# The last 15 full loads of a row-mean kernel, each split by partitions over two DMA queues

## The chip, the core and the metric

The kernel runs on one core of a Trainium2 chip. The metric is the time of one execution in device microseconds (us): the lower the better. Times before are given as the median of three executions; a profile is one further execution, recorded by the hardware profiler.

A core has a memory of 128 partitions (SBUF), engines that work on it (VectorE, written DVE in the profile; ScalarE, ACT; GpSimd, POOL; SyncE, SP) and 16 DMA engines that move data between the chip's main memory (DRAM) and SBUF. An engine issues a DMA into its queue and goes on; the DMA reports its end by adding 16 to a semaphore, on which other engines wait.

## The reference

```python
def setup_inputs():
    return {
        "x": np.random.randn(64, 256, 8192).astype(np.float32),
    }

def reference(x: np.ndarray) -> np.ndarray:
    return np.mean(x, axis=2)
```

There are 64 x 256 = 16384 rows of 8192 numbers, 32 KB each, 536.87 MB in all; the result is one mean for each row, 64 KB in all.

## The kernel before, in words

**Tiling.** Each of the 128 partitions owns 128 rows (`OWN`). The rows are laid out in three zones (`ZONE = [95, 17, 16]` rows per partition), inside each of which a partition's rows follow one another in DRAM. A *full load*, numbered g, brings two rows into each partition: a tile of 128 x 16384 numbers, 64 KB for each partition, 8.39 MB. There are 63 such pairs (g = 0 to 62, `NB`), and one last pair that comes in five chunks. Pair g = 0 holds the odd row of zones 0 and 1 and comes in three pieces. `PAIRS0` is 47: g = 1 to 47 come from zone 0, g = 48 to 62 from zones 1 and 2.

**Buffers.** Three buffers (`bufs`, `NBUF = 3`) take the loads in turn; load g goes to buffer g mod 3. So up to three loads are in flight or being reduced.

**SyncE** issues every DMA of the kernel, in this order: the three pieces of g = 0 and the loads 1 and 2 (lines 107 to 114); in a loop of 15 rounds (`ROUNDS`) over the three buffers the loads 3 to 47 (lines 118 to 123), each after `free_sems[b]` says that VectorE has reduced what lay in the buffer, and that semaphore is counted down again; then, unrolled, the 15 loads 48 to 62 (lines 124 to 127), each after a wait on the same semaphore, which is now left to count up; then the five chunks of the last pair (lines 128 to 133) into the first buffer and a small tile `fin`, and at the end the stores of the result (lines 134 to 142).

**VectorE** reduces each landed load by one `tensor_reduce` to two sums per partition in `res`: the first 60 loads in a loop of 20 rounds (lines 165 to 173), in which the wait on `in_sems[b]` counts that semaphore down, and the loads 60 and 61 unrolled (line 178). Load 62 and the chunks are added by `halves` (line 151), which adds the two halves of a row elementwise and accumulates the sum.

**ScalarE** only takes a part of each of the four larger chunks (lines 202 to 207), after that chunk's semaphore. **GpSimd** scales the finished sums by 1/8192 (lines 87 to 99) when VectorE has done load 60 and what follows it up to row 126; the last column is scaled with the last addition.

What sets the order around the change: the loads go through SyncE's one queue in the order of g; a load is issued when VectorE has finished load g - 3; the chunks are issued when load 60 has been reduced; ScalarE's program holds nothing before its work on the chunks.

## Time and profile before

| what | before |
|---|---|
| median of 3 executions | 1243.22 us (1243.2 to 1243.32) |
| the profiled execution | 1243.06 us |
| its span in the trace | 1241.7 us |
| read from DRAM | 536.87 MB, 432 GB/s over the span |
| ScalarE busy | 5.2 us |
| GpSimd busy | 2.9 us |

The span runs from the first to the last recorded instruction; the execution's own time is 1.36 us longer. In the profile a line such as `L168` is the kernel's line 168. A group of instructions is shown with its engine, operation, output and input tile and count, then its busy time in us, the mean in ns of one, and the idle time of the engine just before them with what ended it. `SPq` or `DVEq` stands for an engine's sequencer, which executes waits and issues DMAs. Of three numbers with strokes between them the first is the least, the second the median, the third the largest, in ns for an instruction. In a table by stretches stand the stretch's bounds and length, the busy time of each engine (with the count of instructions), the clock granted to TensorE, which this kernel does not use, the mean busy share of the 16 DMA engines, and what they moved in GB/s.

### The profile page before, as it was taken

Reading aid. Unit: us, or ns where it says so; the run is one execution under the profiler, and the core shown is the slowest. Engines: PE = TensorE matmul, PEld = TensorE weight load, DVE = VectorE, ACT = ScalarE, POOL = GpSimd, SP = SyncE. Lnnn points to the kernel's source line nnn. Section 1 sums busy time; section 2 is a strip of 40 time slices with the busy share of each in tenths; the row PEclk is TensorE's granted clock in tenths of the full one; section 3 lists DMA queues with packets and bytes.
Section 4 is the critical chain, followed back from the end, with each engine's and each line's share of the span. In section 5 each row is a group of like instructions: output and inputs, shape, how many; then the busy total and the mean of one; then the engine's idle time right before and its main releaser. Section 6 shows DMA issues by size and latency. Waiting matters only on the chain. (4 is left out here: it accounts for less than half of the span.)

```text
span 1241.7 us, 549 instructions
## 1 busy us (share of the span) xinstructions
DVE 1084.1 (87%) x76; ACT 5.2 (0%) x9; POOL 2.9 (0%) x9
## 2 busy tenths in 40 slices
DVE  2898988989889898898898988989889898898987
ACT  0000000000000000000000000000000000000001
POOL 0000000000000000000000000000000000000000
DMA  9999999999999999999999999999999999999998
GB/s 405 439 439 439 439 435 410 439 439 439 439 439 433 412 439 439 439 439 439 426 418 439 439 439 439 439 422 422 439 439 439 439 439 422 422 439 439 439 439 374
DMA packets 10512, 536.94 MB, mean 432 GB/s; under 512 B 1552, under 2 KB 1552, under 8 KB 1936
## 3 DMA queue, kind: packets, MB, share of 16 engines
q1 hardware_dynamic: 10512, 536.94, 99.9%
HBM read 536.87 MB, written 0.07 MB: 432 GB/s over the span
## 5 line engine op out<-in xcount | busy, mean ns | idle before, releaser
L168 DVE TENSOR_REDUCE res<-buf 128x16384 f32 x60 | 1033.2, 17220 | 146.5 <-DVEq L167 146.5
L178 DVE TENSOR_REDUCE res<-buf 128x2 f32<-128x16384 f32 x2 | 34.4, 17220 | 4.0 <-DMA buf<-in_x_dram 4.0
L151 DVE CUSTOM_DVE_ANT_0 buf<-buf 128x4096 f32<-128x4096 f32 (+3 forms) x6 | 16.0, 2672 | 5.4 <-DMA buf<-in_x_dram 5.4
L207 ACT ACTIVATE buf<-buf 128x928 f32<-128x928 f32 (+3 forms) x4 | 3.6, 897 | 1233.7 <-DMA buf<-in_x_dram 1233.7
L97 POOL TENSOR_SCALAR scaled<-res 128x94 f32<-128x94 f32 (+2 forms) x3 | 2.4, 784 | 1235.0 <-DVE res L151 1234.8
L207 ACT ACT_TABLE_LOAD x1 | 1.3, 1283 | 0.7 <-PEq L221 0.7
L207 ACT ACTIVATION_READ_ACCUMULATOR buf<-buf 128x1 f32 x4 | 0.7, 187 | 0.0
L151 DVE CUSTOM_DVE_ANT_0 fin<-fin 128x260 f32<-128x260 f32 x1 | 0.4, 429 | 0.3 <-DMA fin<-in_x_dram 0.3
L97 POOL TENSOR_SCALAR ends<-res 128x15 f32<-128x15 f32 x1 | 0.3, 264 | 0.1
L151 DVE DVE_READ_ACCUMULATOR2_ANT res<- 128x1 f32 x3 | 0.3, 84 | 0.0
L151 DVE DVE_READ_ACCUMULATOR2_ANT fin<- 128x1 f32 x3 | 0.2, 81 | 0.0
L221 POOL MEMSET const-bfloat16-1.0<- 128x1 bf16 x1 | 0.1, 102 | 0.0
L221 POOL MEMSET const-uint8-127<- 128x1 uint8 x1 | 0.1, 102 | 0.0
L88 POOL MEMSET fin<- 128x1 f32 x1 | 0.1, 99 | 0.3 <-POOLq L221 0.3
L221 POOL MEMSET const-float32-0.0<- 128x1 f32 x1 | 0.1, 99 | 0.2 <-issue 0.2
L221 POOL MEMSET const-float32-1.0<- 128x1 f32 x1 | 0.1, 99 | 0.0
L151 DVE DVE_READ_ACCUMULATOR2_ANT ends<- 128x1 f32 x1 | 0.1, 82 | 0.0
## 6 DMA issues: line engine op xcount, KB each, us to landing
buf<-in_x_dram SPq DMA_DIRECT2D x1, 4560.0 KB, 32.2
buf<-in_x_dram SPq DMA_DIRECT2D x1, 4096.0 KB, 20.6
buf<-in_x_dram SPq DMA_DIRECT2D x1, 3072.0 KB, 11.4
buf<-in_x_dram SPq DMA_DIRECT2D x1, 2240.0 KB, 37.1
buf<-in_x_dram SPq DMA_DIRECT2D x1, 1024.0 KB, 4.6
buf<-in_x_dram SPq DMA_DIRECT2D x62, 40.3
buf<-in_x_dram SPq DMA_DIRECT2D x1, 768.0 KB, 38.5
buf<-in_x_dram SPq DMA_DIRECT2D x1, 368.0 KB, 39.0
```

The lines of the kernel that those rows point to most:

```text
L88: eng.memset(part(NPART - 1), 0.0).then_inc(part_d, 1)
L97: eng.tensor_scalar(dst, src, inv, None, op0=mybir.AluOpType.mult).then_inc(pool_sem, 1)
L151: eng.tensor_tensor_reduce(ap[:, 0:n], ap[:, 0:n], ap[:, n : 2 * n], scale=scale, scalar=0.0, op0=ADD, op1=ADD, accum_out=to,).then_inc(do ...
L168: eng.tensor_reduce(sums[:, bass.ds(i, 1), b, :], bufs[b][:].rearrange("p (j l) -> p j l", j=2), X, ADD,).then_inc(free_sems[b], 1)
L178: eng.tensor_reduce(res[:, 2 * g : 2 * g + 2], bufs[b][:].rearrange("p (j l) -> p j l", j=2), X, ADD,).then_inc(free_sems[0] if b == 0 els ...
L207: eng.activation(ap, ap, COPY, accum_out=part(c)).then_inc(part_a, 1)
L221: nc = _bacc.Bacc("TRN2", target_bir_lowering=False, num_devices=1)
```

## The change

The 15 loads g = 48 to 62 each become two DMAs. Partitions 0 to 63 are issued by SyncE, as before, partitions 64 to 127 by ScalarE, each after its own wait for the buffer. Both add 16 to the same new semaphore `late_in_sems[b]`, so VectorE waits for multiples of 32; VectorE's releases for these loads go to the new `late_free_sems[b]`. Since constants are waited for there, VectorE's loop is shortened from 20 to 15 rounds (`ROUNDS`), and loads 45 to 62 are unrolled. Loads 0 to 47, the chunks and the stores stay as they are, on SyncE's queue. ScalarE's 15 issues stand ahead of its work on the chunks.

```diff
+        late_in_sems = [sem(f"late_in_sem{i}") for i in range(NBUF)]
+        late_free_sems = [sem(f"late_free_sem{i}") for i in range(NBUF)]
...
         eng = nc.gpsimd
         eng.memset(part(NPART - 1), 0.0).then_inc(part_d, 1)
-        eng.wait_ge(free_sems[0], LOADS0 + 1)
+        eng.wait_ge(late_free_sems[0], LOADS0 + 1)
         eng.wait_ge(owned_sem, 4)
...
         eng = nc.sync
...
         for g in range(PAIRS0 + 1, NB):
             b = g % NBUF
-            eng.wait_ge(free_sems[b], (g - PAIRS0 - 1) // NBUF + 1)
-            eng.dma_start(bufs[b][:], rows_of(first_row(g), 2)).then_inc(in_sems[b], 16)
-        eng.wait_ge(free_sems[0], LOADS0 + 1)
+            eng.wait_ge(late_free_sems[b], (g - PAIRS0 - 1) // NBUF + 1)
+            eng.dma_start(bufs[b][0 : P // 2, :], rows_of(first_row(g), 2)[0 : P // 2, :]).then_inc(
+                late_in_sems[b], 16
+            )
+        eng.wait_ge(late_free_sems[0], LOADS0 + 1)
         two = rows_of(2 * NB, 2)
...
-        with eng.Fori(0, NB // NBUF - 1) as i:
+        with eng.Fori(0, ROUNDS) as i:
             for b in range(NBUF):
                 eng.wait_ge(in_sems[b], 16).then_inc(in_sems[b], -16)
                 eng.tensor_reduce(
...
                 ).then_inc(free_sems[b], 1)
-        for b in range(NBUF):
-            g = NB - NBUF + b
-            eng.wait_ge(in_sems[b], 16)
-            if b < 2:
+        for g in range(ROUNDS * NBUF, NB):
+            b = g % NBUF
+            if g <= PAIRS0:
+                eng.wait_ge(in_sems[b], 16)
+            else:
+                eng.wait_ge(late_in_sems[b], 32 * ((g - PAIRS0 - 1) // NBUF + 1))
+            if g < NB - 1:
                 eng.tensor_reduce(
                     res[:, 2 * g : 2 * g + 2],
                     bufs[b][:].rearrange("p (j l) -> p j l", j=2),
                     X,
                     ADD,
-                ).then_inc(free_sems[0] if b == 0 else owned_sem, 1)
+                ).then_inc(late_free_sems[b] if g < NB - 2 else owned_sem, 1)
             else:
...
         eng = nc.scalar
+        for g in range(PAIRS0 + 1, NB):
+            b = g % NBUF
+            eng.wait_ge(late_free_sems[b], (g - PAIRS0 - 1) // NBUF + 1)
+            eng.dma_start(bufs[b][P // 2 : P, :], rows_of(first_row(g), 2)[P // 2 : P, :]).then_inc(
+                late_in_sems[b], 16
+            )
         for c in range(4):
             eng.wait_ge(chunk_sems[c], 16)
```

More of the change, by code (lines that the diff above doesn't have):

```diff
@@ L83, in bass_global_avg_pool_1d_kernel, with rows_of @@
         part = lambda n: fin[:, LAST + n : LAST + n + 1]
+        def rows_of(n, k):
+            z = 2 if n >= FROM[2] else 1 if n >= FROM[1] else 0
+            return zone[z][:, (n - FROM[z]) * L : (n - FROM[z] + k) * L]
         eng = nc.gpsimd
         eng.memset(part(NPART - 1), 0.0).then_inc(part_d, 1)
-        eng.wait_ge(free_sems[0], LOADS0 + 1)
+        eng.wait_ge(late_free_sems[0], LOADS0 + 1)
         eng.wait_ge(owned_sem, 4)
@@ L102, in bass_global_avg_pool_1d_kernel @@
         eng = nc.sync
-        def rows_of(n, k):
-            z = 2 if n >= FROM[2] else 1 if n >= FROM[1] else 0
-            return zone[z][:, (n - FROM[z]) * L : (n - FROM[z] + k) * L]
         a, z = rows_of(ZONE[0] - 1, 1), rows_of(ZONE[0], 1)
```

## The prediction

> **What bounds the kernel now.** I read the page first: busy times, slices, queues, costliest groups.

> ```profile
> span 1241.7 us, 549 instructions
> ...
> DVE 1084.1 (87%) x76; ACT 5.2 (0%) x9; POOL 2.9 (0%) x9
> ...
> DMA  9999999999999999999999999999999999999998
> ...
> DMA packets 10512, 536.94 MB, mean 432 GB/s; under 512 B 1552, under 2 KB 1552, under 8 KB 1936
> ## 3 DMA queue, kind: packets, MB, share of 16 engines
> q1 hardware_dynamic: 10512, 536.94, 99.9%
> ...
> L168 DVE TENSOR_REDUCE res<-buf 128x16384 f32 x60 | 1033.2, 17220 | 146.5 <-DVEq L167 146.5
> L178 DVE TENSOR_REDUCE res<-buf 128x2 f32<-128x16384 f32 x2 | 34.4, 17220 | 4.0 <-DMA buf<-in_x_dram 4.0
> ```

> VectorE is busy 87% of the span, the DMA engines 99.9%: the transfers set the time. All of them stand in one queue, q1. The packet counts give the size of a packet: 10512 less the 1936 under 8 KB is 8576, which is 67 x 128, that is, the 62 full loads (g = 1 to 62) and five large pieces (three at the start, chunks 0 and 1) at one packet for each partition. So a full load is 128 packets of 64 KB, eight for each of 16 engines.

> Then busy times by stretch, cut at the ends of the loads that the change touches:

> ```profile
> core 0: us, DVE busy (x) ACT busy (x) POOL busy (x), PEclk, DMA share, GB/s
> 22.50:911.30 888.80, 792.11 (x46) 0.00 (x0) 0.00 (x0) 1.00 1.00 434
> 911.30:930.60 19.30, 17.22 (x1) 0.00 (x0) 0.00 (x0) 1.00 1.00 435
> 930.60:1220.20 289.60, 258.30 (x15) 0.00 (x0) 0.00 (x0) 1.00 1.00 433
> 1220.20:1241.70 21.50, 16.44 (x14) 3.96 (x8) 2.62 (x4) 1.00 0.87 366
> ```

> The 15 loads of the change, g = 48 to 62, take 289.60 us, 19.31 each, at a DMA share of 1.00 and 433 GB/s. One 64 KB packet on one engine is 19.31 / 8 = 2.41 us. What follows the last of them is 21.5 us long. And the order of events where the change begins and ends:

> ```profile
> 909.31 270.74 SPq L127 DMA_DIRECT2D buf<-in_x_dram  x15
> 911.37 17.22 DVE L168 TENSOR_REDUCE res<-buf 128x16384 f32 x1 [2.09 <-DVEq L167]
> 930.65 17.22 DVE L168 TENSOR_REDUCE res<-buf 128x16384 f32 x1 [2.06 <-DVEq L167]
> 949.96 17.22 DVE L168 TENSOR_REDUCE res<-buf 128x16384 f32 x1 [2.09 <-DVEq L167]
> ...
> 1200.96 17.22 DVE L178 TENSOR_REDUCE res<-buf 128x2 f32<-128x16384 f32 x1 [2.16 <-DMA buf<-in_x_dram]
> 1220.27 4.42 DVE L151 CUSTOM_DVE_ANT_0 buf<-buf 128x4096 f32<-128x4096 f32 x1 [2.09 <-DMA buf<-in_x_dram]
> ```

> VectorE starts on g = 46 at 911.37, on g = 47 at 930.65, on g = 48 at 949.96, on g = 62 at 1220.27. It idles about 2.1 us before each, waiting for data. (Inside the loop the wait is put on its own sequencer, DVEq; the two unrolled reductions show the same wait as DMA.)

> **The change part by part.** *Issues and waits.* SyncE still issues 15 DMAs here, and ScalarE 15 more.

> ```profile
> L127 SPq DMA_DIRECT2D buf<-in_x_dram x15: 327/328/339, 909.3 to 1179.7; - x15
> ...
> DMA to landing us min/median/max: 40.4/40.5/40.5
> ```

> ```profile
> SPq L127 <- DVE res L168: 284.2, 15, 19.0
> ```

> ```profile
> ACT buf L207 <- DMA buf<-in_x_dram: 1233.7, 4, 1229.0
> ```

> An issue takes 0.33 us and then the load needs 40.5 us to land, since two loads stand ahead of or in it: 2 x 19.31 = 38.6, and 1.8 for getting started and reporting. SyncE waits up to 19.0 us between issues for VectorE. ScalarE does nothing until 1229, so 15 issues of 0.33 to 0.43 us and the waits before them cost nothing: queued behind them stand only the four ACTIVATEs of the chunks (L207), which in program order follow the last issue, and whose data comes later still. If that cover were gone, 15 x 0.43 = 6.5 us of ScalarE would show. VectorE's shorter loop (15 rounds instead of 20), its constant waits and its other semaphores touch sequencer work inside the 2.1 us idle time before each load: nothing. GpSimd waits for the same reduction under another name: nothing. Fifteen more sets of 16 completion packets are 15 more packets per engine, under 512 B each; at the 27.1 GB/s of one engine (64 KB in 2.41 us) at most 0.02 us each, 0.3 us in all.

> *Bytes.* The same 8.39 MB move per load, but in two transfers of 64 partitions, and the trace has no 64-partition transfer of any size. The price is bounded from both sides. Below: a half costs half of a full load, 9.66 us, because only the bytes count; 15 x (2 x 9.66 - 19.31) = 0. A gain beyond that is limited by the share of 1.00: see the third rival. Above: a half costs as much as a full load, 19.31 us, because what is limited is the rate into each set of partitions, and a half load brings each of its partitions the same 64 KB. Then 15 x (2 x 19.31 - 19.31) = 289.6 us.

> I take the upper end. The nearest row is the full load itself: same queue kind, same packets of 64 KB per partition, and a rate that stands at 433 to 435 in every stretch, as a limit of fixed width would leave it. My hypothesis is that this width belongs to the partitions: the lower 64 can take half of it (217 GB/s), the upper 64 the other half. A full load asks both halves equally. A half load asks one, and is as slow as a full one unless the other half load runs beside it on the other engines.

> That last condition decides, so I follow the packets. I assume that a half load too is spread over all 16 engines, four packets on each, and that an engine with work on both queues takes whole packets from them in turn. Up to 909 all engines work one queue through packets of equal length, and 99.9% of 16 x 1241.7 us is filled: 1.2 us idle per engine, less than what the start and the end of the span take (0.7 us pass before the first issue), so no engine is far ahead of another. They enter the new stage in step: all 16 write a ScalarE packet (upper partitions), then all 16 a SyncE packet (lower partitions), each time at half rate, 4.83 us a packet instead of 2.41. Two engines that share one half-width equally finish together and stay together; nothing pulls them apart. Every half load then pays 4 x 2.41 = 9.66 us extra, wherever it falls in the order, and 30 of them pay 289.6.

> [...]

> *Order.* ScalarE's queue is empty when it gets its half of g = 48 at 909, while SyncE's still holds the rest of g = 46 and all of g = 47. So the upper halves run one load ahead: g = 47 shares its turns with the upper halves of 48 and 49 and lands after 4 x (4.83 + 2.41) x 2 = 58 us, near 969 instead of 930. VectorE stands idle meanwhile; that costs nothing while the engines have work, and they have: halves of 48 and 49 are waiting. At the end the last lower half (g = 62) runs alone, at half rate as well. No packet is priced twice, so the sum is not changed by the order.

> *Sum.* Against the profiled execution: span 1241.7 + 289.6 + 0.3 = 1531.6 us. That execution took 1243.06 in all, 1.36 us outside the span, and lies 0.16 below the median of 1243.22; I forecast **1533 us**. In stretches: the 15 loads end near 1510 instead of 1220.2, and the 21.5 us after them stay. The forecast's own range is 1500 (the engines a tenth of a packet out of step, 289.6 x 0.9) to 1560 (each load also shows its 1.8 us start, 15 x 1.8 = 27).

> **The rivals.** *Only the bytes count.* If each engine is limited by itself, or each half lands on eight engines of its own, the two halves side by side take 19.31 us. For: the engines are filled to 1.00, as one would see with that limit too. Against: nothing in the trace, only that the widths of both would have to be equal by accident. The one new wait: g = 47 shares its turns and lands at 930.6 + 19.3 = 949.9; VectorE frees its buffer 17.2 us later, at 967.2, and the queues run dry at 949.9 + 19.3 = 969.2, with 1.8 us needed to start. So at most about 1 us is lost, and VectorE regains its 19.3 us of delay at 2.1 per load over 13 loads. Result 1243 to 1245.

> *Out of step.* The partition limit holds, but one engine of a sharing pair gets ahead, or engines interleave in pieces smaller than a packet. Then engines write to opposite halves and most of the loss vanishes. A floor remains where the two queues don't balance: 12.6 of the 16.8 MB moved beside g = 47 go to the upper half, 57.9 us instead of 38.6, so +19.3; then the lower half of 48 alone, +9.7; the lower half of 62 alone, +9.7. That is 1282; with half of the packets colliding, 1243 + 145 = 1388. For: equal sharing is my assumption, a small bias would add up over 120 packets. Against: the regular 19.3 us steps of VectorE show no drift in the whole span. Range 1262 (one of the two imbalances of 19.3 us only) to 1500.

> *Faster.* A second queue lets an engine fetch the next packet while the first queue's is finishing. Place: the seam between two packets. Price: the slices of the profile move at most 439 GB/s against 433 here.

> ```profile
> GB/s 405 439 439 439 439 435 410 439 439 439 439 439 433 412 439 439 439 439 439 426 418 439 439 439 439 439 422 422 439 439 439 439 439 422 422 439 439 439 439 374
> ```

> At 439 a load takes 19.11 us, 15 save 15 x 0.20 = 3 us: 1240. It decides only if halves don't slow each other at all and there are seams; a share of 1.00 and a chain of full packets leave hardly any (the dips between the 439s are whole packets counted in the next slice).

> **How the numbers follow.** A measurement of this kernel tells about 0.2% (2.5 us) from no change. Chances: forecast (1500 to 1560) 0.53; out of step (1262 to 1500) 0.27; only the bytes count 0.14; faster 0.03; slower than 1560, where two queues also get in each other's way, 0.03. Slower is 0.53 + 0.27 + 0.03 = 0.83, same 0.14, faster 0.03. The range 1262 to 1560 holds the first two, 0.80.

> **What would show it.** In the profile after: a second queue with 15 x 64 = 960 packets of 64 KB and 63 MB; in the stretch of the split loads 215 to 220 GB/s at a DMA share still near 1.00 (packets take 4.8 us, engines are not idle); VectorE's starts 38.6 us apart with some 21.4 us idle, and one idle time near 40 us before g = 47; landing times of the split halves near 77 us from SyncE and 40 to 60 from ScalarE; the last 21.5 us unchanged. A stretch at 433 GB/s with starts 19.3 us apart says that only bytes count. Something between, drifting from 38 to 20 us, says that the engines fall out of step. Idle DMA engines in the stretch would prove the reasoning wrong altogether: then a wait, not a width, is the cause.

## The result, and the profile after

The changed kernel takes 1554.33 us (median of 4; 1553.91 to 1555.16) against 1243.21 us before in the same series: 1.2504 times as long, 95% interval 1.2488 to 1.2519, or 311 us more. The forecast was 1533.

The page of the changed kernel, the lines that answer to those shown of before:

```profile
span 1552.6 us, 519 instructions
...
DVE 1084.0 (70%) x76; ACT 5.2 (0%) x9; POOL 2.9 (0%) x9
...
DMA  9999999999999999999999999999999999999999
GB/s 431 434 432 432 432 432 432 432 432 432 432 432 432 432 432 444 446 434 432 432 432 432 432 378 245 214 216 216 214 191 216 216 216 201 204 216 216 216 194 294
DMA packets 10752, 536.94 MB, mean 346 GB/s; under 512 B 1792, under 2 KB 1792, under 8 KB 2176
## 3 DMA queue, kind: packets, MB, share of 16 engines
q1 hardware_dynamic: 9552, 474.03, 80.7%
q10 hardware_dynamic: 1200, 62.92, 19.2%
...
L172 DVE TENSOR_REDUCE res<-buf 128x16384 f32 x45 | 774.9, 17220 | 115.3 <-DVEq L171 115.3
L185 DVE TENSOR_REDUCE res<-buf 128x2 f32<-128x16384 f32 x17 | 292.7, 17220 | 345.1 <-DMA buf<-in_x_dram 345.1
```

The same bytes move, and the DMA engines are as full as before (9 in every slice); VectorE's busy time is unchanged. The rate falls in the 24th slice, in which the split loads begin, and is about half from the 25th on. The second queue, q10, has 62.92 MB in 1200 packets, 960 of 64 KB and 240 under 512 B, 16 for each of its 15 DMAs. Full engines at half the rate mean that each packet takes about twice as long: by the packets' durations in the two traces 4.99 us in the mean of the 1920 of the split loads, where before it was 2.42. Nothing stands idle waiting for an order.

VectorE's instructions in order of time show where the 311 us lie (g = 46 to 49 and 60 to 62):

```profile
911.48 17.22 DVE L185 TENSOR_REDUCE res<-buf 128x2 f32<-128x16384 f32 x1 [2.09 <-DMA buf<-in_x_dram]
962.61 17.22 DVE L185 TENSOR_REDUCE res<-buf 128x2 f32<-128x16384 f32 x1 [33.91 <-DMA buf<-in_x_dram]
997.66 17.22 DVE L185 TENSOR_REDUCE res<-buf 128x2 f32<-128x16384 f32 x1 [17.83 <-DMA buf<-in_x_dram]
1037.51 17.22 DVE L185 TENSOR_REDUCE res<-buf 128x2 f32<-128x16384 f32 x1 [22.63 <-DMA buf<-in_x_dram]
...
1475.90 17.22 DVE L185 TENSOR_REDUCE res<-buf 128x2 f32<-128x16384 f32 x1 [22.63 <-DMA buf<-in_x_dram]
1510.79 17.22 DVE L185 TENSOR_REDUCE res<-buf 128x2 f32<-128x16384 f32 x1 [17.67 <-DMA buf<-in_x_dram]
1531.36 4.42 DVE L155 CUSTOM_DVE_ANT_0 buf<-buf 128x4096 f32<-128x4096 f32 x1 [3.35 <-DMA buf<-in_x_dram]
```

The reduction of g = 47, a load that is not itself split, starts 32 us late (962.61 against 930.65), because the upper halves of 48 and 49 take turns with it: between 915 and 952 us the packets of the two queues start mostly in turns of 16, q10's taking 4.7 to 4.9 us each, q1's 2.6 to 2.8. From g = 49 to g = 60 a load takes (1475.90 - 997.66) / 12 = 39.85 us instead of 19.31. The steps are the same for g = 49 to 55, whose rows come from zone 1, and for g = 56 to 60 from zone 2, so where the rows lie in DRAM is not seen to matter. Load 62 starts at 1531.36 instead of 1220.27: 311.1 us, the whole loss. What follows it takes 21.2 us, before 21.4.

### The profile page after: what moved, and what is told of

It is laid out like the page before. It is cut to its first block, busy times and chain, and to the rows that moved or that the text cites. A ratio compares the mean times of both kernels' runs of the same rounds, so it can differ in the third digit from the quotient of the medians.

```text
span 1552.6 us, 519 instructions
## 1 busy us (share of the span) xinstructions
DVE 1084.0 (70%) x76; ACT 5.2 (0%) x9; POOL 2.9 (0%) x9
## 2 busy tenths in 40 slices
DMA packets 10752, 536.94 MB, mean 346 GB/s; under 512 B 1792, under 2 KB 1792, under 8 KB 2176
## 3 DMA queue, kind: packets, MB, share of 16 engines
q10 hardware_dynamic: 1200, 62.92, 19.2%
## 5 line engine op out<-in xcount | busy, mean ns | idle before, releaser
L172 DVE TENSOR_REDUCE res<-buf 128x16384 f32 x45 | 774.9, 17220 | 115.3 <-DVEq L171 115.3
L185 DVE TENSOR_REDUCE res<-buf 128x2 f32<-128x16384 f32 x17 | 292.7, 17220 | 345.1 <-DMA buf<-in_x_dram 345.1
```

Source lines behind the costliest of these rows:

```text
L172: eng.tensor_reduce(sums[:, bass.ds(i, 1), b, :], bufs[b][:].rearrange("p (j l) -> p j l", j=2), X, ADD,).then_inc(free_sems[b], 1)
L185: eng.tensor_reduce(res[:, 2 * g : 2 * g + 2], bufs[b][:].rearrange("p (j l) -> p j l", j=2), X, ADD,).then_inc(late_free_sems[b] if g < N ...
```

## The experiments

All are edits of the changed kernel in its 15 split loads, unless said otherwise; `row` stands for `rows_of(first_row(g), 2)`, and VectorE's wait, mostly not shown, is set to 16 for each DMA of a load. The questions are: is it the partitions or the two queues, how fine is the division, which half lands first, and does it matter that the engines are in step.

**Two queues, split by columns.**

```diff
-            eng.dma_start(bufs[b][0 : P // 2, :], row[0 : P // 2, :])      # SyncE
+            eng.dma_start(bufs[b][:, 0:L], row[:, 0:L])
...
-            eng.dma_start(bufs[b][P // 2 : P, :], row[P // 2 : P, :])      # ScalarE
+            eng.dma_start(bufs[b][:, L : 2 * L], row[:, L : 2 * L])
```

> The 15 loads are split by columns, 128 partitions each, again one half from each queue. If the limit is the rate into each half of the partitions (my theory), every packet finds its full width: starts of VectorE 19.3 us apart, 1243 to 1246 us in all. If two queues that work side by side disturb each other, whatever they carry: 1554 us as with the change.

It took 1247.78 us, 1.0037 times the kernel before (1.0023 to 1.0052). By stretches of the span (busy times of VectorE, ScalarE, GpSimd, clock, DMA share, GB/s):

```profile
911.30:930.60 19.30, 17.22 (x1) 0.00 (x0) 0.00 (x0) 1.00 0.94 407
930.60:1220.20 289.60, 251.12 (x15) 1.28 (x1) 0.00 (x0) 1.00 1.00 433
1220.20:1246.40 26.20, 23.20 (x15) 3.96 (x8) 2.88 (x4) 1.00 0.76 323
```

Two queues side by side carry 433 GB/s, as one did. So the queues are not the cause. The 4.6 us that it does lose lie in the tail: the third stretch is 26.2 us where the kernel before needs 21.5, at a DMA share of 0.76 instead of 0.87. VectorE finishes late, after the data: it starts g = 47 at 940.27 instead of 930.65, and still waits some 2.1 us for almost every later load, so that it does not catch up.

**Both halves on one queue; quarters on one queue.**

```diff
+            for i in range(n):                    # n = 2, and in a second kernel n = 4
+                s = slice(i * P // n, (i + 1) * P // n)
+                eng.dma_start(bufs[b][s, :], row[s, :]).then_inc(late_in_sems[b], 16)   # SyncE; ScalarE issues none
```

> The same two halves by partitions, both issued by SyncE, lower half first. My theory: all engines write one half at a time, 8 packets of 4.9 to 5.1 us for a load, 39.5 to 41 us a load, 1550 to 1570 us in all. If two queues are the cause: 1243 us.

> Each of the 15 loads as four DMAs of 32 partitions on SyncE's queue. My theory: a quarter uses the width of the half in which it lies, 2 packets of about 5 us for each engine, 40 us a load, 1550 to 1570 us. If the rate goes with the number of partitions in the DMA, a quarter gets a quarter of the rate: 77 us a load, 2110 us.

1563.09 and 1562.73 us (1.2574 and 1.2571 times before). A stretch inside the split loads, the two halves first, then the four quarters:

```profile
960.00:1200.00 240.00, 103.32 (x6) 0.00 (x0) 0.00 (x0) 1.00 1.00 207
```

```profile
960.00:1200.00 240.00, 103.32 (x6) 0.00 (x0) 0.00 (x0) 1.00 1.01 208
```

The loss is there without a second queue, and it is not proportional to the number of partitions in a DMA: 32 get what 64 get. Against 207 GB/s on one queue, the changed kernel moves 211 to 213 on two:

```profile
1000.00:1200.00 200.00, 86.84 (x6) 0.00 (x0) 0.00 (x0) 1.00 1.01 211
1200.00:1450.00 250.00, 114.18 (x7) 0.00 (x0) 0.00 (x0) 1.00 1.01 213
```

**Another 64 partitions.**

```diff
+            for s in (slice(32, 96), slice(0, 32), slice(96, 128)):
+                eng.dma_start(bufs[b][s, :], row[s, :]).then_inc(late_in_sems[b], 16)   # SyncE; ScalarE issues none
```

> Each of the 15 loads as three DMAs on SyncE's queue: partitions 32 to 95, 0 to 31 and 96 to 127. My theory: the middle 64 lie half in each half of the partitions, so its 4 packets for each engine run at 2.42 us, 9.7 us together; the outer two stay within one half, 2 packets of about 5 us each, 20 us together; 29.7 us a load, 1243 + 15 x 10.4 = 1399 us (1385 to 1415). If any DMA of fewer than 128 partitions runs at a rate that goes with their number (or if 64 partitions are slow wherever they lie), the middle one takes 20 us as well: 40 us a load or more, 1554 us or more.

> The kernel with partitions 32 to 95, 0 to 31 and 96 to 127 once more, since its two executions took 1404 and 1461 us. If there are two ways in which the engines can fall into step, the times stand in two groups near these two; if the 1461 us was a chance disturbance, nearly all are at 1404 us. My theory of the width asks that none is near 1554 us.

Of the eight executions six took 1403.64 to 1413.43 us, two 1460.38 and 1460.73. VectorE in one of the first kind:

```profile
1050.69 17.22 DVE L185 TENSOR_REDUCE res<-buf 128x2 f32<-128x16384 f32 x1 [12.76 <-DMA buf<-in_x_dram]
1080.67 17.22 DVE L185 TENSOR_REDUCE res<-buf 128x2 f32<-128x16384 f32 x1 [12.76 <-DMA buf<-in_x_dram]
```

A load takes 29.98 us, as expected from 9.7 for partitions 32 to 95 and 20 for the rest. Sixty-four partitions are not slow as such: cut into 0 to 63 and 64 to 127, the same load takes 39.85 us in the changed kernel. The second group of times, 57 us above the first, is not explained.

**How fine is the division?** Three kernels, all on SyncE's queue: partitions 32 to 95 alone, 36 to 99 alone (both leave out the other 64 partitions of each load), and eight DMAs of 16.

```diff
+            s = slice(32, 96)                     # second kernel: slice(36, 100)
+            eng.dma_start(bufs[b][s, :], row[s, :]).then_inc(late_in_sems[b], 16)
...
+            for i in range(8):                    # third kernel
+                s = slice(16 * i, 16 * i + 16)
+                eng.dma_start(bufs[b][s, :], row[s, :]).then_inc(late_in_sems[b], 16)
```

> Each of the 15 loads brings partitions 32 to 95 only, on SyncE's queue; the other partitions are left out and reduced from what lay in the buffer. The 4 packets for each engine take 2.42 us as in the kernel with three pieces, 9.7 us a load, so VectorE becomes the bound at 17.3 us a load: 1243 - 15 x 2.06 = 1212 us (1208 to 1220), DMA share in the stretch some 0.56, near 243 GB/s.

> The same with partitions 36 to 99: only the four partitions 32 to 35 are given up for 96 to 99. My first theory (each half of the partitions takes half the rate): 28 of the 64 are lower and 36 upper, nine sixteenths in the busier half, packets of 2.7 us, 11 us a load, VectorE is the bound as before, 1212 us. [...]

> Each of the 15 loads as eight DMAs of 16 partitions on SyncE's queue; nothing is left out. First theory (halves): an eighth uses the width of the half in which it lies, 40 us a load, 1563 us as with two or four pieces. [...]

They took 1207.56, 1270.85 and 2069.2 us, in one execution each. The first lies a little below the range expected (1208 to 1220), the second and the third above the 1212 and 1563 that a division into halves gives. A stretch of each, in that order:

```profile
960.00:1100.00 140.00, 140.00 (x9) 0.00 (x0) 0.00 (x0) 1.00 0.59 240
```

```profile
960.00:1100.00 140.00, 117.77 (x8) 0.00 (x0) 0.00 (x0) 1.00 0.57 204
```

```profile
960.00:1100.00 140.00, 34.44 (x2) 0.00 (x0) 0.00 (x0) 1.00 1.00 112
```

With 32 to 95, VectorE is busy 140 of 140 us: the loads are no longer the bound. Moved on by four partitions, the same number of bytes keeps VectorE waiting (117.77 of 140), and the engines are still only 0.57 busy: a part of the packets holds up the load while most of the engines are done. Short slices show how many. These are of 1 us, from 1020 us, and a packet counts in the slice in which it starts:

```profile
GB/s 0 918 0 66 66 0 0 0 66 66 0 0 0 918 131 0 721 197 131 918 0 786 131 66 66 0 0 0 66 66 0 0 0 721 328 0 328 590 66 983
```

66 GB/s is one packet of 64 KB: again and again two packets start alone, 5 us after the two before them, while nothing else starts. The packets' own durations in the trace confirm it: between 975 and 1150 us one in eight takes 5.06 us, the others 2.42 in the median. One in eight is what two engines of 16 carry, if the packets are spread evenly. Such packets rule out a division into two halves only, by which this kernel too would have been bound by VectorE. Its steps are 20.2 us:

```profile
994.83 17.22 DVE L183 TENSOR_REDUCE res<-buf 128x2 f32<-128x16384 f32 x1 [3.00 <-DMA buf<-in_x_dram]
1015.07 17.22 DVE L183 TENSOR_REDUCE res<-buf 128x2 f32<-128x16384 f32 x1 [3.01 <-DMA buf<-in_x_dram]
1035.29 17.22 DVE L183 TENSOR_REDUCE res<-buf 128x2 f32<-128x16384 f32 x1 [3.00 <-DMA buf<-in_x_dram]
```

or four packets of 5.06 us. The kernel takes 27.6 us more than the one before, whose steps are 19.3; 11.5 of them come with the last load, which VectorE starts on at 1248.32, 30.8 us after g = 61, and this is not explained. Sixteen consecutive partitions get 112 GB/s, near a quarter of 434, where a half gets 207. So the division is finer than two halves; which partitions belong together is not shown.

**Which half lands first.** A semaphore for each half:

```diff
-                late_in_sems[b], 16               # ScalarE's DMA
+                upper_in_sems[b], 16
...
-                eng.wait_ge(late_in_sems[b], 32 * ((g - PAIRS0 - 1) // NBUF + 1))
+                eng.wait_ge(late_in_sems[b], 16 * ((g - PAIRS0 - 1) // NBUF + 1))
+                eng.wait_ge(upper_in_sems[b], 16 * ((g - PAIRS0 - 1) // NBUF + 1))
```

> The changed kernel with a semaphore of its own for each half, so that the landing of the two halves can be told apart. My theory: upper halves run a load ahead of lower ones, since ScalarE's queue was empty when SyncE's still held g = 47; halves from ScalarE land 50 to 65 us after their issue, halves from SyncE 95 to 105. The profile of the changed kernel, where both halves report to one semaphore, reads the other way round (52 for SyncE, 102 for ScalarE); if that is true, SyncE's land first here too. Time 1554 us either way.

1556.62 us in one execution. First the changed kernel's two issuing lines, then the same two here; the last line of each is the time from issue to landing:

```profile
L129 SPq DMA_DIRECT2D buf<-in_x_dram x15: 465/466/542, 909.4 to 1453.3; - x15
...
DMA to landing us min/median/max: 37.5/52.4/53.7
```

```profile
L213 ACTq DMA_DIRECT2D buf<-in_x_dram x15: 496/498/567, 909.4 to 1453.3; - x15
...
DMA to landing us min/median/max: 78.0/102.3/108.8
```

```profile
L130 SPq DMA_DIRECT2D buf<-in_x_dram x15: 465/466/542, 909.2 to 1455.0; - x15
...
DMA to landing us min/median/max: 78.1/102.4/110.2
```

```profile
L215 ACTq DMA_DIRECT2D buf<-in_x_dram x15: 497/497/568, 909.2 to 1455.0; - x15
...
DMA to landing us min/median/max: 38.4/52.5/55.1
```

The upper halves run a load ahead: they land 52.5 us after their issue in the median, the lower ones 102.4. With one semaphore for both, the profile reads the wrong way round, as if it gave the first count to the first issue.

**Does it matter that the engines are in step?** Three kernels try to make eight of the 16 engines late, well ahead of the split loads. The first two do it with load g = 1 (w, 16 KB or 8 KB of columns for each partition, is meant for those eight engines alone); the third adds a small DMA, of 8 partitions with 8 KB each, ahead of load g = 3.

```diff
+        eng.dma_start(bufs[1][0:112, :], one[0:112, :])              # 112 packets of 64 KB
+        eng.dma_start(bufs[1][112:128, 0 : 2 * L - w], one[112:128, 0 : 2 * L - w])
+        eng.dma_start(bufs[1][112:120, 2 * L - w :], one[112:120, 2 * L - w :])   # meant for 8 engines
+        eng.dma_start(bufs[1][120:128, 2 * L - w :], one[120:128, 2 * L - w :])   # meant for the same 8
...
+        eng.dma_start(lag[0:8, :], z[0:8, 0:FIRST])                  # third kernel, instead
```

> The changed kernel, but load g = 1 is divided so that eight of the 16 engines carry 32 KB more than the other eight and run half a packet (1.2 us) late from then on. Nothing is changed in the 15 split loads. My theory (both engines of a pair that shares a half's width are in the same half at the same time): now they meet for half of each packet, which then takes the mean of 2.42 and 4.95, 3.7 us; some 29.5 us a load instead of 39.9, with stretches of one queue alone as slow as before: 1400 to 1430 us. If the step of the engines doesn't matter, and a half load is slow in itself: 1554 us.

> The same with 16 KB, a quarter of a packet late. My theory: the engines of a pair meet for three quarters of a packet, 4.3 us, 34.5 us a load, 1475 to 1495 us. If the step doesn't matter: 1554 us.

> [...] All loads are as in the changed kernel, so the slow opening that the earlier late kernels had (a DMA of 112 partitions) is gone. [...] If the late kernels before showed the rule (a lag brings little, 4.3 to 4.8 us a packet): 1500 to 1556 us.

They took 1574.03 us (1571.11 to 1576.8), 1530.87 and 1552.09 us, and 1575.22 us. The last is above the 1500 to 1556 expected. To see whether the engines were late, look at slices of 1 us again: the kernel before from 960 us, the changed kernel from 960, the half-packet kernel from 880, the third kernel from 880.

```profile
GB/s 0 1049 0 1049 0 0 1049 0 1049 0 524 524 0 1049 0 983 66 0 1049 0 1049 0 328 721 0 1049 0 852 197 0 1049 0 1049 0 0 1049 0 1049 0 655
```

```profile
GB/s 983 66 0 0 0 852 197 0 0 0 983 66 0 0 0 983 66 0 0 0 983 66 0 0 0 983 66 0 0 0 852 197 0 0 0 852 197 0 0 0
```

```profile
GB/s 459 459 262 524 459 459 524 197 459 524 459 459 393 393 393 459 459 524 524 131 524 524 393 524 393 393 393 459 459 459 524 197 524 459 459 524 197 459 524 459
```

```profile
GB/s 197 0 1049 0 1049 0 328 721 0 1049 0 786 262 0 1049 0 983 66 66 983 0 1049 0 459 590 0 1049 0 918 131 0 1049 0 1049 0 0 0 0 0 262
```

1049 GB/s is 16 packets of 64 KB in one microsecond: before, 16 packets start together, every 2.4 us, and in the split loads of the changed kernel every 5 us. In the half-packet kernel the starts are spread over the time of a packet (131 to 524 GB/s in every slice); the engines are out of step, if not in two groups of eight. In the third kernel 16 start together: the small DMA did not do what it was meant to. The half-packet kernel, g = 46 to 49, 59, 60 and 62:

```profile
934.78 17.22 DVE L201 TENSOR_REDUCE res<-buf 128x2 f32<-128x16384 f32 x1 [2.09 <-DMA buf<-in_x_dram]
1012.10 17.22 DVE L201 TENSOR_REDUCE res<-buf 128x2 f32<-128x16384 f32 x1 [60.10 <-DMA buf<-in_x_dram]
1047.84 17.22 DVE L201 TENSOR_REDUCE res<-buf 128x2 f32<-128x16384 f32 x1 [18.52 <-DMA buf<-in_x_dram]
1086.45 17.22 DVE L201 TENSOR_REDUCE res<-buf 128x2 f32<-128x16384 f32 x1 [21.39 <-DMA buf<-in_x_dram]
...
1459.32 17.22 DVE L201 TENSOR_REDUCE res<-buf 128x2 f32<-128x16384 f32 x1 [18.85 <-DMA buf<-in_x_dram]
1495.34 17.22 DVE L201 TENSOR_REDUCE res<-buf 128x2 f32<-128x16384 f32 x1 [18.80 <-DMA buf<-in_x_dram]
...
1550.77 4.42 DVE L161 CUSTOM_DVE_ANT_0 buf<-buf 128x4096 f32<-128x4096 f32 x1 [6.71 <-DMA buf<-in_x_dram]
```

It reaches g = 46 23.3 us late, from its slow opening. From there to g = 62 it needs 616.0 us, the changed kernel 619.9, so in all almost nothing is won. But this is the sum of two effects. g = 47 comes 26 us later still, and the later loads win that back: they are cheaper, 36.0 to 38.6 us each instead of 39.85, though far from the 29.5 expected. In the quarter-packet kernel's profiled execution (1530.87 us) the same way takes 574.2 us, a gain of 46, where some 70 were expected; g = 55 and 56 are shown between its ends:

```profile
933.70 17.22 DVE L201 TENSOR_REDUCE res<-buf 128x2 f32<-128x16384 f32 x1 [2.09 <-DMA buf<-in_x_dram]
...
1278.43 17.22 DVE L201 TENSOR_REDUCE res<-buf 128x2 f32<-128x16384 f32 x1 [18.17 <-DMA buf<-in_x_dram]
1313.85 17.22 DVE L201 TENSOR_REDUCE res<-buf 128x2 f32<-128x16384 f32 x1 [18.20 <-DMA buf<-in_x_dram]
...
1507.94 4.43 DVE L161 CUSTOM_DVE_ANT_0 buf<-buf 128x4096 f32<-128x4096 f32 x1 [4.07 <-DMA buf<-in_x_dram]
```

A load takes 35.4 us there, where 34.5 were expected; but its second execution is 21 us longer. Nor is it shown that g = 47 comes late because of the lag: in the third kernel, whose packets still start together at 900 us, it comes at 995.06, 32 us after that of the changed kernel:

```profile
995.06 17.22 DVE L189 TENSOR_REDUCE res<-buf 128x2 f32<-128x16384 f32 x1 [65.98 <-DMA buf<-in_x_dram]
```

So a split load is 3 to 10% shorter in the half-packet kernel, whose starts are spread, where 26% were expected, and 11% in the quarter-packet kernel, whose starts are not shown. The trace does not say which engine carries a packet, so whether the engines that hinder each other were apart in these kernels is not shown either.

## Why the prediction was right, and where it was not

*The bound.* Right. The DMA engines were full before, and are full after at half the rate.

*Issues, waits, other engines.* Right at nothing. ScalarE's 15 issues of 0.50 us and its table load of 1.28, now at 1453 us, lie where nobody waits for them.

*The price of a half load.* Direction right, division too coarse, size too low. The rate depends on the partitions that a DMA fills: cut by columns the loads move at 433 GB/s, cut into 0 to 63 and 64 to 127 at 207 to 213, and with 32 to 95 alone they no longer bound the kernel (VectorE 140 of 140 us). The division is finer than the two halves of the prediction, as 36 to 99 (four packets of 5.06 us) and the eighths (112 GB/s) show; what it is that limits the rate is not shown, and that a width belongs to the partitions remains the author's hypothesis. The term that was off is the 4.83 us for a packet. By the packets' own durations in the trace, the 1920 packets of the split loads take 4.99 us in the mean. That is 2.57 more than the 2.42 of a packet before, where 2.41 was taken, and with 30 x 4 = 120 packets for each engine in the mean it makes 308 of the 311.1 us. The 0.16 us by which it exceeds the 2.41 make 19 of the 21 us between forecast and result. A packet of a half load takes a little more than double, more so after a packet to the same half: from 965 to 1453 us in the changed kernel a packet takes 4.95 us after one to the other half, 5.11 after one to the same. That fits 5.07 us at 207 GB/s on one queue (16 x 65.5 KB / 207), 4.95 at 212 on two. The 1.8 us start of a load, which set the upper end of the range, is not the reason: the DMA share stays at 0.99 to 1.01 in the split loads.

*"That last condition decides."* Neither shown nor refuted. The engines of the changed kernel were indeed in step, as the prediction argued: 16 packets start within 2 us, every 5 us. But where the starts were spread, in the half-packet kernel, a split load still took 36.0 to 38.6 us. So the condition of the rival "out of step" was not met in the changed kernel, and its price was not reached where it was (1574.03 us): 1282 to 1388 us do not come about. Whether a half load is free when the other half runs beside it is open; no run here isolates a pair of engines.

*The order.* Right: g = 47 at 962.61, forecast 969; upper halves a load ahead. Landing times of ScalarE's halves were put at 40 to 60 us (52.5), SyncE's at 77 (102.4): a lower half waits for more than two loads' time.

*Only the bytes count.* Refuted for partitions; it holds for columns, at 1247.78 instead of 1243 to 1245, since VectorE does not make up its delay as supposed. *Faster* did not occur in any run that moves all bytes.

## What to carry to other kernels

## What was not expected of the hardware

- Partitions 32 to 95 load at nearly the full rate (a DMA share of 0.59 at 240 GB/s is 2.58 us for a packet, in a full load 2.42) and 36 to 99 do not: four partitions make the difference between a load that VectorE outlasts and one of 20.2 us.
- Engines out of step were little better off. With starts spread over the time of a packet, a split load took 36.0 to 38.6 us (half-packet kernel) instead of 39.85.
- Three DMAs of 64, 32 and 32 partitions fall into one of two times, 1404 to 1413 or 1460 us, with the same code; why is open.
- In the half-packet kernel a DMA of 112 partitions ran far below the full rate as well, at 264 GB/s (the second stretch is almost all its own):

```profile
2.00:20.00 18.00, 0.00 (x0) 0.00 (x0) 0.00 (x0) 1.00 1.01 431
20.00:52.00 32.00, 17.22 (x1) 0.00 (x0) 0.00 (x0) 1.00 1.11 264
```
